# RWKV block of a four-layer trunk: four weight matrices split into two parts during the feed-forward ahead of it, and a new order for the scan's work

## The chip, the cores and the metric

One core of one Trainium2 chip runs the whole program in one launch. The metric is the device time of that launch in microseconds (us). A table below has the times of the kernel before.

## What is computed

The reference is a trunk of four layers on 256 context tokens and 256 latent tokens of width 1024. Layer 0 and layer 3 mix tokens with a gated linear recurrence (HGRN2), layer 1 with RWKV-7, layer 2 with latent attention, and each layer ends in a convolutional feed-forward part. The change touches the feed-forward of layer 0 and the RWKV mixer of layer 1:

```python
def conv_ffn(h, w_in, w_conv, b_conv, w_out):
    a, v = jnp.split(h @ w_in, 2, axis=-1)
    a = lax.conv_general_dilated(a, w_conv[:, None, :], ...) + b_conv
    return (jax.nn.silu(a) * v) @ w_out

def rwkv7_scan(r, w, k, v, kk, a, s0):
    def step(S, inp):
        rt, wt, kt, vt, kkt, at = inp
        sa = jnp.einsum('bhvk,bhk->bhv', S, -kkt)
        S = S * wt[:, :, None, :] + sa[..., None] * (kkt * at)[:, :, None, :] + vt[..., None] * kt[:, :, None, :]
        return S, jnp.einsum('bhvk,bhk->bhv', S, rt)
    ...

def project(h):                      # inside rwkv7_mixer
    ...
    r = heads(x_r @ w_rkv[0])
    k = heads(x_k @ w_rkv[1])
    v = heads(x_v @ w_rkv[2])
    g = jax.nn.sigmoid(x_g @ g1) @ g2
    ...
# readout: ((normalised y + bonus) * g) @ w_o, for both directions of the scan
```

Beside each layer the modulation of a later layer is computed: `silu(c) @ w_mod[layer] + b_mod[layer]`, a product with a matrix of 1024 x 6144.

## The kernel before

Activations lie transposed in SBUF, width on the 128 partitions and the 512 tokens along the free axis (tiles `xT`). Products in fp32 are made from three products of rounded parts: every weight and activation is split into a high part (`hi`, type fp32r) and the rest (`lo`), and `mm3` (L430) adds `hi*hi`, `hi*lo` and `lo*hi`. For weights that is done on the fly by `weights` (L414): SP loads 512 KB into `wraw` (four buffers), ACT casts it to `whi` (L426), DVE subtracts to `wlo` (L427), three buffers each.

**Feed-forward** (`ffn`, L2082): two rounds over column blocks, in each some steps over `w_in` (two blocks of columns for the gate, two for the value, 96 products of 128x512) and four over `w_out`. While it runs, `mod` loads 256 KB tiles of the next layer's `w_mod` on the SP queue (L391), eight to a step, in the first twelve steps.

**RWKV projections** (`rw_project`, L869): a norm, the six mixed inputs (`mix`), low-rank products, and two full products by `dense4`: first the keys, then the receptance. Each loads its matrix in eight chunks through `weights`, 24 products of 128x512 to a chunk. Results go to DRAM (`rwk`, `rwr`).

**RWKV scan** (`rw_scan`, L1037): the values' product (`values`, L1814) in 16 units of 12 products, whose weights come by `load` (L1821, tile `vr`), `high` (ACT, L1825) and `low` (DVE, L1829); then eight pairs of 128-column blocks, four for the context tokens and four for the latent ones. Of each pair, both directions are scanned in chunks of 64 tokens: `scaled` makes decays and keys, `products` (L1311) the chunk matrices `G`, which go through DRAM (`dg`, `inv`, `zd`) for a triangular inversion on DVE (L1404), `merge` completes the inverse on PE, `chain` runs the four dependent chunks (L1535 `r`, L1573 `v`, L1585 `k`, L1597 new state), and `readout` norms, gates and multiplies by the output matrix: SP loads `ow` (L1721), ACT makes `owh` (L1725), GpSimd (POOL) `owl` (L1729), PE the product. Between all that `modulation` (L1865) makes the modulation of two later layers in 96 units: SP loads 512 KB into `mraw`, which has one buffer (L1871), and PE makes four products of it (L1878, tile `md`).

**What sets the order.** In the feed-forward and the projections the framework orders each engine's instructions. In the scan the order is fixed by a planner in the kernel: every piece of work is a job on one engine, with a cost and a lag from `RW_COST`, delays between engines from `RW_LAT`, and a due place from the table `RW_AT`; `Jobs.schedule` (L143) simulates the engines and emits the jobs in the order of their planned starts. Each engine, and the SP and POOL queues of DMAs, then runs its own list strictly in that order. Rings (`jobs.rings`) give the number of buffers of each kind of tile. For the load of `mraw` the table has a cost of 1.46 and a lag of 1.2.

Of the kernel before, what the change touches and what calls it, by code (L numbers as in the profile page):

```python
# [51 lines left out]
RW_OW = 2  # L52
RW_M = 40
RW_LAT = {("PE", "PE"): 0, ("PE", "DVE"): 0.2, ("PE", "Act"): 0.2, ("PE", "Pool"): 0.2, ("PE", "SP"): 1.3,
          ("DVE", "PE"): 0.2, ("DVE", "DVE"): 0.127, ("DVE", "Act"): 0.13, ("DVE", "Pool"): 0.1, ("DVE", "SP"): 1.3,
          ("Act", "PE"): 0.26, ("Act", "DVE"): 0.2, ("Act", "Act"): 0.143, ("Act", "Pool"): 0.2, ("Act", "SP"): 1.3,
          ("Pool", "PE"): 0.26, ("Pool", "DVE"): 0.2, ("Pool", "Act"): 0.2, ("Pool", "Pool"): 0, ("Pool", "SP"): 1.3,
          ("SP", "PE"): 0, ("SP", "DVE"): 0, ("SP", "Act"): 0, ("SP", "Pool"): 0, ("SP", "SP"): 0}
RW_COST = {"end": 0.01, "vload": (0.73, 1.2), "vhigh": 0.52, "vlow": 0.6, "vmm": (2.62, 0.0, 6144), "vkeep": 0.48, "vout": (0.73, 1.2),
           "load": (3.6, 1.2), "norms": (0.23, 0.0, 512), "key": 0.79, "gate": (0.46, 0.0, 768), "tanh": 0.72, "affine": 0.34, "decays": 0.6,  # L60
           "exp": 0.52, "exp2": 0.62, "mul": 1.23, "ka": 0.6, "bmul": 0.6, "loadw": (0.82, 1.2), "high": 0.52, "low": 1.23,
           "heads": (0.46, 0.0, 1024), "product": (0.87, 0.0, 1024), "mask": 0.6, "out": (0.73, 1.2), "ktok": (0.43, 0.0, 512), "tok": 0.72,
           "gather": (2.3, 1.0), "ones": 0.04, "iout": (5.3, 1.5), "pair": (1.07, 0.0, 256), "keepw": 0.4, "corner": 0.63, "bturn": 0.34,
           "mfirst": (0.64, 0.0, 140), "g0": 1.04, "half": 0.53, "copy": 0.49, "turn": (0.56, 0.0, 512), "vtok": 0.8, "r": (0.29, 0.0, 512),
           "R": 0.16, "v": (0.29, 0.0, 256), "Sv": 0.32, "k": (0.29, 0.0, 512), "new": 0.78, "yg": (0.29, 0.0, 512), "sc": 0.72,
           "yx": (0.29, 0.0, 256), "yhigh": 0.52, "ylow": 0.6, "sums": (0.46, 0.0, 1024), "rs2": (3.6, -1.28), "rs3": 1.92,
           "g2": (0.92, 0.0, 1984), "wload": (0.73, 1.2), "whigh": 0.52, "wlow": 1.23, "oproj": (1.36, 0.0, 3072), "oadd": 0.6, "aout": (1.0, 1.5),
           "fin": 1.09, "xload": (0.73, 1.2), "yload": (0.73, 1.2), "res": 0.79, "mload": (1.46, 1.2), "mod": (0.49, 0.0, 1024), "mkeep": 0.48,
           "mtr": (0.43, 0.0, 512), "madd": 0.5}
RW_MAN = ("PE", "DVE", "Activation", "Pool", "SP")  # L70
RW_AT = {
# [50 lines left out]
class Jobs:  # L122
# [8 lines left out]
    def add(self, engine, name, fn, deps=(), takes=(), uses=(), tag=None, cost=None):  # L131
# [8 lines left out]
        self.list.append(x)  # L140
        return x

    def schedule(self, places, stage, lat, ordered, eps=0.05):  # L143


        free, live, ready, order = {}, {r: [] for r in self.rings}, [], []
# [2077 lines left out]
```

## Time and profile before

| | us |
|---|---|
| three runs: median (lowest to highest) | 3205.2 (3204.08 to 3209.22) |
| the profiled execution, device time | 3206.3 |
| its span, first to last instruction | 3204.4 |
| busy in the span: PE / DVE / ACT / POOL | 2886.2 / 1780.7 / 1396.0 / 496.9 |
| DMA queue of SP: data and share of the 16 engines | 377.29 MB, 38.4% |

The profile is of one execution. PE is the engine of matrix products, PEld its loading of weights, DVE, ACT and POOL the vector, scalar and GpSimd engines, SPq the DMA queue of SP. PEclk is the clock that was granted to PE, as a share of 2.4 GHz; its other level is 1.2 GHz. In lists of waits, "A <- B" says that A sat idle until B was done. In lists of groups, the idle time before a group and what ended it stand behind the bar. POOL issues no DMA in this kernel.

### The profile page before, as it was taken

Reading aid. Unit: us, or ns where it says so; the run is one execution under the profiler, and the core shown is the slowest. Engines: PE = TensorE matmul, PEld = TensorE weight load, DVE = VectorE, ACT = ScalarE, POOL = GpSimd, SP = SyncE. Lnnn points to the kernel's source line nnn. Section 1 sums busy time; section 2 is a strip of 40 time slices with the busy share of each in tenths; the row PEclk is TensorE's granted clock in tenths of the full one; section 3 lists DMA queues with packets and bytes.
Section 4 is the critical chain, followed back from the end, with each engine's and each line's share of the span. In section 5 each row is a group of like instructions: output and inputs, shape, how many; then the busy total and the mean of one; then the engine's idle time right before and its main releaser. Section 6 shows DMA issues by size and latency. Waiting matters only on the chain. (4 is left out here: it accounts for less than half of the span.)

```text
span 3204.4 us, 52055 instructions
## 1 busy us (share of the span) xinstructions
PE 2886.2 (90%) x20861; PEld 2307.1 (72%) x20861; DVE 1780.7 (56%) x3081; ACT 1396.0 (44%) x2642; POOL 496.9 (16%) x567
## 2 busy tenths in 40 slices
PE   7999999999679777878768999899989999999898
PEld 4588877778557556666547888776678887888898
DVE  4277764334674547666636434466554344488765
ACT  3266543223443345555444323245433233477544
POOL 1023200000332325344420000000000000023000
PEclk9999999999789867877878999999989999999999
DMA  7522145553264644554542333210123322322454
GB/s 277 194 68 66 51 147 171 192 158 104 81 194 133 184 126 131 154 148 139 155 140 82 96 99 96 83 48 27 40 80 99 99 92 86 93 81 81 149 184 132
DMA packets 438466, 381.33 MB, mean 119 GB/s; under 512 B 94396, under 2 KB 395346, under 8 KB 438098
## 3 DMA queue, kind: packets, MB, share of 16 engines
q1 hardware_dynamic: 436848, 377.29, 38.4%
q8 instruction: 164, 2.69, 0.4%
q10 hardware_dynamic: 1378, 0.73, 0.1%
q14 instruction: 76, 0.62, 0.1%
HBM read 354.89 MB, written 22.54 MB: 118 GB/s over the span
## 5 line engine op out<-in xcount | busy, mean ns | idle before, releaser
L427 DVE TENSOR_TENSOR wlo<-wraw,whi 128x1024 fp32r<-128x1024 f32 (+1 forms) x408 | 486.3, 1194 | 546.5 <-ACT whi L426 534.9
L433 PE MATMUL mm<-hl,whi 128*128 128x512 f32 (+1 forms) x2024 | 744.5, 368 | 10.2 <-DVE hl L528 10.2
L432 PE MATMUL mm<-hh,whi 128*128 128x512 f32 (+1 forms) x2024 | 744.1, 372 | 10.3 <-ACT hh L527 6.9
L434 PE MATMUL mm<-hh,wlo 128*128 128x512 f32 (+1 forms) x2024 | 741.0, 367 | 0.0
L426 ACT CAST whi<-wraw 128x1024 fp32r<-128x1024 f32 (+1 forms) x408 | 412.2, 1013 | 753.0 <-PE mm L433 668.0
L432 PEld LDWEIGHTS mm<-hh,whi 128*128 128x128 f32 x2024 | 385.4, 191 | 91.0 <-issue 10.0
L433 PEld LDWEIGHTS mm<-hl,whi 128*128 128x128 f32 x2024 | 385.4, 190 | 78.2 <-DVE hl L528 13.6
L434 PEld LDWEIGHTS mm<-hh,wlo 128*128 128x128 f32 x2024 | 385.1, 190 | 65.9 <-issue 6.1
L432 PE MATMUL mm<-uh,whi 128*128 128x512 f32 (+1 forms) x704 | 255.2, 363 | 0.0
L433 PE MATMUL mm<-ul,whi 128*128 128x512 f32 (+1 forms) x704 | 255.1, 363 | 0.0
L434 PE MATMUL mm<-uh,wlo 128*128 128x512 f32 (+1 forms) x704 | 254.2, 363 | 0.0
L488 POOL TENSOR_TENSOR t<-t,t 128x512 f32<-128x512 f32 (+1 forms) x27 | 35.0, 1298 | 902.8 <-ACT t L484 887.0
L1878 PE MATMUL md<-mraw,sc 128*32 128x256 f32 x768 | 74.4, 465 | 86.1 <-DMA mraw<-in_w_mod_dram 85.7
L432 PEld LDWEIGHTS mm<-uh,whi 128*128 128x128 f32 x704 | 132.7, 189 | 23.9 <-issue 2.5
L433 PEld LDWEIGHTS mm<-ul,whi 128*128 128x128 f32 x704 | 132.9, 189 | 20.4
L434 PEld LDWEIGHTS mm<-uh,wlo 128*128 128x128 f32 x704 | 132.5, 189 | 20.7
L2111 DVE SCALAR_TENSOR_TENSOR t<-mm,prm,t 128x510 f32<-128x510 f32 (+1 forms) x88 | 60.0, 682 | 139.5 <-ACT t L2109 139.5
L2109 ACT ACTIVATE t<-mm,prm 128x512 f32<-128x512 f32 (+1 forms) x88 | 63.2, 718 | 147.0 <-PE mm L434 147.0
L542 DVE SCALAR_TENSOR_TENSOR xT<-mm,mod,xT 128x256 f32<-128x256 f32 x176 | 74.6, 478 | 92.1 <-PE mm L434 92.1
L701 POOL TENSOR_TENSOR t<-t 128x512 f32<-128x512 f32 x32 | 46.4, 1449 | 361.0 <-DVE t L691 317.7
L2118 DVE TENSOR_TENSOR t<-t,mm 128x512 f32<-128x512 f32 (+1 forms) x88 | 54.4, 620 | 84.5 <-PE mm L434 84.3
L1878 PEld LDWEIGHTS md<-mraw,sc 128*32 128x32 f32 x768 | 16.5, 118 | 105.8 <-DMA mraw<-in_w_mod_dram 95.8
(418 smaller groups left out, 5167.5 us busy)
## 6 DMA issues: line engine op xcount, KB each, us to landing
wraw<-in_ffn_w_in_dram SPq DMA_DIRECT2D x176, 512.0 KB
mraw<-in_w_mod_dram SPq DMA_DIRECT2D x192, 256.0 KB
mraw<-in_w_mod_dram SPq DMA_DIRECT2D x96, 512.0 KB
wraw<-in_hg_w_in_dram SPq DMA_DIRECT2D x80, 512.0 KB
wraw<-in_ffn_w_out_dram SPq DMA_DIRECT2D x80, 512.0 KB
wraw<-in_rw_w_rkv_dram SPq DMA_DIRECT2D x16, 512.0 KB
w<-wg SPq DMA_DIRECT2D x8, 1024.0 KB
ow<-in_rw_w_o_dram SPq DMA_DIRECT2D x32, 256.0 KB
```

What stands on the lines that cost most here:

```text
L426: nc.scalar.copy(h, r)
L427: nc.vector.tensor_tensor(out=w, in0=r, in1=h.bitcast(F32), op=ALU.subtract)
L432: nc.tensor.matmul(ps, lhsT=wh, rhs=xh, start=start, stop=False)
L433: nc.tensor.matmul(ps, lhsT=wh, rhs=xl, start=False, stop=False)
L434: nc.tensor.matmul(ps, lhsT=wl, rhs=xh, start=False, stop=stop)
L488: (nc.gpsimd if k < 4 else nc.vector).tensor_tensor(out=acc[:, lo:hi], in0=acc[:, lo:hi], in1=sq[:, lo:hi], op=ALU.add)
L542: nc.vector.scalar_tensor_tensor(out=self.xT[n][:, sl], in0=ps[:, sl], scalar=m[:, which * 8 + n, s:s + 1], in1=self.xT[n][:, sl], op0=ALU ...
L701: nc.gpsimd.tensor_tensor(out=c3(de), in0=b3[:, :, end:end + 1].to_broadcast([P, 8, 64]), in1=b3, op=ALU.subtract)
L1878: nc.tensor.matmul(g["ps"][32 * c:32 * c + 32, halves[f]], lhsT=self.sc[:, k, :], rhs=g["raw", u][:, c], start=k == 0 and f == 0, stop=k = ...
L2109: nc.scalar.activation(c[:, sl], pa[b][:, sl], AF.Identity, bias=self.prm[:, cb + j + b:cb + j + b + 1], scale=w[1])
L2111: nc.vector.scalar_tensor_tensor(out=c3[:, :, 1:], in0=p3[:, :, :255], scalar=w[0], in1=c3[:, :, 1:], op0=ALU.mult, op1=ALU.add)
L2118: nc.vector.tensor_tensor(out=ss[b][:, sl], in0=ss[b][:, sl], in1=pv[b][:, sl], op=ALU.mult)
```

## The change

1. `presplit`, new: during the feed-forward of layer 0, 64 steps split the matrices of keys, receptance, values and output ahead of their use. A step loads 128x512 (256 KB) on the POOL queue into `praw`, ACT casts it to `phi`, DVE subtracts to `plo`, and two DMAs on the POOL queue store both to DRAM (`prek`, `prer`, `prev`, `preo`). `praw` and `plo` have one buffer, `phi` two.
2. `dense4`, `values` and the readout load both parts from there, with two DMAs where there was one, and no longer cast or subtract.
3. The planner gets new costs, lags and delays, a rule that keeps some DVE jobs from a start while POOL is busy (`RW_LOCK`), another threshold in its model of PE's clock, and a new table `RW_AT`; `mraw` gets a second buffer; the jobs `vhigh`, `vlow`, `whigh`, `wlow` are gone.

```diff
-RW_LAT = {("PE", "PE"): 0, ("PE", "DVE"): 0.2, ("PE", "Act"): 0.2, ("PE", "Pool"): 0.2, ("PE", "SP"): 1.3,
+RW_LAT = {("PE", "PE"): 0, ("PE", "DVE"): 0.05, ("PE", "Act"): 0.08, ("PE", "Pool"): 0.08, ("PE", "SP"): 0.05,
...
+RW_LOCK = ("affine", "bmul", "inv", "ka.0", "ka.1", "key.1", "key.2", "mask.11", "res", "rs3")
...
-                speed = 1.0 if k > 0 and busy.get(k - 1, 0.0) >= 3060 else 0.5
+                speed = 1.0 if k > 0 and busy.get(k - 1, 0.0) >= 2750 else 0.5
...
+            if x.engine == "DVE" and (x.name in locks or x.kind in locks):
+                t = max(t, port[0])
...
+    def presplit(self, st):
+
+        nc, a = self.nc, self.a
+        pool = st.enter_context(self.tc.tile_pool(name="pre", bufs=2, reuse_waits="tile"))
+        self.pre = {}
+        for n, w in (("k", a["rw_w_rkv"][0, 1]), ("r", a["rw_w_rkv"][0, 0]), ("v", a["rw_w_rkv"][0, 2]), ("o", a["rw_w_o"][0])):
+            self.pre[n] = self.dr.tile([P, 2, KT, D], F32, tag=f"pre{n}", name=f"pre{n}", bufs=1)
+            for k in range(KT):
+                for c in (slice(0, NT), slice(NT, D)):
+                    raw = pool.tile([P, NT], F32, tag="praw", name="praw", bufs=1)
+                    hi = pool.tile([P, NT], F32R, tag="phi", name="phi")
+                    lo = pool.tile([P, NT], F32R, tag="plo", name="plo", bufs=1)
+                    nc.gpsimd.dma_start(out=raw, in_=w[k * P:(k + 1) * P, c])
+                    nc.scalar.copy(hi, raw)
+                    nc.vector.tensor_tensor(out=lo, in0=raw, in1=hi.bitcast(F32), op=ALU.subtract)
+                    nc.gpsimd.dma_start(out=self.pre[n][:, 0, k, c], in_=hi.bitcast(F32))
+                    nc.gpsimd.dma_start(out=self.pre[n][:, 1, k, c], in_=lo.bitcast(F32))
+                    yield
...
+        def two(n, k0, n0):
+
+            _, hi, lo = (t.rearrange("p (a b) -> p a b", b=NT) if t is not None else t for t in self.wtiles(False))
+            for i, t in enumerate((hi, lo)):
+                nc.sync.dma_start(out=t.bitcast(F32), in_=self.pre[n][:, i, k0:k0 + 2, n0:n0 + NT])
+            return hi, lo
...
-                    wh, wl = self.weights(w[:, k0:k0 + 2, n0:n0 + NT], 2, NT)
+                    wh, wl = two(name, k0, n0)
...
-                w = g["w", u] = lp().tile([P, 2, 256], F32, tag="ow", name="ow", bufs=2)
-                nc.sync.dma_start(out=w, in_=a["rw_w_o"][0].rearrange("(k p) n -> p k n", p=P)[:, p0:p0 + 2, 256 * u:256 * u + 256])
+                w = g["w", u] = lp().tile([P, 2, 2, 256], F32R, tag="ow", name="ow", bufs=RW_OW)
+                for i in range(2):
+                    nc.sync.dma_start(out=w[:, i].bitcast(F32), in_=self.pre["o"][:, i, p0:p0 + 2, 256 * u:256 * u + 256])
...
-                x_ = V["wh"] = job("Act", "whigh", lambda u=u: whigh(u), [x_] + ([V["wh"]] if "wh" in V else []), [wh], [w])
-                x_ = job("Pool", "wlow", lambda u=u: wlow(u), [x_], [], [w, wh])
...
+                g["w", x] = vp.tile([P, 2, 4, P], F32R, tag="vw", name="vw", bufs=RW_VW)
+                for i in range(2):
+                    nc.sync.dma_start(out=g["w", x][:, i].bitcast(F32), in_=self.pre["v"][:, i, 4 * (x % 2):4 * (x % 2) + 4, x // 2 * P:x // 2 * P + P])
...
-                a_ = job("Act", "vhigh", lambda x=x: high(x), [a_], [h], [r])
-                a_ = job("DVE", "vlow", lambda x=x: low(x), [a_], [], [r, h])
...
-                t = g["raw", u] = sp.tile([P, 4, 256], F32, tag="mraw", name="mraw", bufs=1)
+                t = g["raw", u] = sp.tile([P, 4, 256], F32, tag="mraw", name="mraw", bufs=2)
...
-    def ffn(self, l, segs, mod=None):
+    def ffn(self, l, segs, mod=None, pre=False):
...
+            spl = self.presplit(st) if pre else iter(())
...
                 for j in range(j0, j1, 2):
                     next(nxt, None)
+                    steps(4)
...
                 for nb in range(0, KT, 2):
                     next(nxt, None)
+                    steps(3)
```

In the new table the load of `mraw` has a cost of 0.4 and a lag of 5.5. The call of `ffn` sets `pre` for layer 0 alone.

**Vector engine, feed-forward of layer 0** (a step over `w_in`; `plo`, `praw`, `phi` are the new split's tiles, `ul` and `uh` the activations' parts). Before:

```order
L2118 TENSOR_TENSOR t_4149<-t_4149,mm 128x512
L2118 TENSOR_TENSOR t_4155<-t_4155,mm 128x512
L427 TENSOR_TENSOR wlo<-wraw,whi 128x1024
```

Now:

```order
L2135 TENSOR_TENSOR t_4185<-t_4185,mm 128x512
L2135 TENSOR_TENSOR t_4191<-t_4191,mm 128x512
L432 TENSOR_TENSOR wlo<-wraw,whi 128x1024
L2139 TENSOR_TENSOR ul<-t_4185,uh 128x512
L2139 TENSOR_TENSOR ul<-t_4191,uh 128x512
L449 TENSOR_TENSOR plo<-praw,phi 128x512
L432 TENSOR_TENSOR wlo<-wraw,whi 128x1024
L449 TENSOR_TENSOR plo<-praw,phi 128x512
```

One new subtraction stands between nearly every two subtractions of feed-forward weights, in the same strict list; five of the 64 stand behind the feed-forward's last one, two of them among the mixed inputs of the projections.

**Tensor engine, end of the values' product** (`w<-xh,vl` and `w<-xh,vw` are its last product; `ax<-X,kb` the chunk matrices, `xg` the decay gates, `md` a modulation unit of four products, `x,G` and `xT,w` the merge of the inverse, `ident,vt` the turning of the values). Before:

```order
L434 MATMUL w<-xh,vl 128x512
L1332 MATMUL ax<-ident,kb_8122 128x128 x4
L1878 MATMUL md<-mraw,sc 32x256 x8
L1311 MATMUL ax<-X,kb_8123 128x128 x8
L1311 MATMUL ax<-X,kb_8122 128x128 x8
L1173 MATMUL ax<-xg_6742,w_8124 128x256
```

Now:

```order
L458 MATMUL w<-xh,vw 128x512
L1899 MATMUL ax<-ident,modev 128x128 x4
L1472 MATMUL ax<-x_9064,G 32x32 x32
L1889 MATMUL md<-mraw,sc 32x256 x4
L1203 MATMUL ax<-xg_7262,w_8612 128x256
L1204 MATMUL ax<-xg_7262,w_8612 128x256
```

The first pair's chunk matrices, 32 products of 128x128, now stand inside the values' product, and with them the inversion that hangs on them: what follows the values is the merge of that inverse. Before, only 16 of them stood there, and 48 (of two pairs) between the values and the chain's first `r`. Modulation units inside the values' product go from 9 to 15, those between it and the first `r` from 7 to 4.

**SP queue, one pair of the scan** (`inv<-dg` brings a pair's matrices to the inversion, `zd<-inv` takes them back; `ow` are the readout's weights). Before:

```order
L1327 DMA inv<-dg 32x16x16 x4
L1871 DMA mraw<-in_w_mod_dram 128x4x256
L1148 DMA xT_85<-rwk 128x2x256
L1149 DMA w_8124<-wg 128x8x256
L1150 DMA xT_87<-rwr 128x2x256
L1871 DMA mraw<-in_w_mod_dram 128x4x256 x2
L1637 DMA g_12350<-wo 128x3x256
```

Now:

```order
L1357 DMA inv<-dg 32x16x16 x4
L1882 DMA mraw<-in_w_mod_dram 128x4x256
L1752 DMA ow<-preo 128x2x256 x2
L1178 DMA xT_85<-rwk 128x2x256
L1179 DMA w_8612<-wg 128x8x256
L1180 DMA xT_87<-rwr 128x2x256
```

Loads of `ow`, two for each, now stand between the inversion's DMAs, where before a later place in the pair held one for each.

## Rows read from the trace of the kernel before

**Rows 1.** The page's first part: busy time, share of the span, instructions

```profile
PE 2886.2 (90%) x20861; PEld 2307.1 (72%) x20861; DVE 1780.7 (56%) x3081; ACT 1396.0 (44%) x2642; POOL 496.9 (16%) x567
```

**Rows 2.** Windows by stage: start:end, length, busy time (instructions) by engine, clock, DMA share, GB/s

```profile
486.00:820.00 334.00, 334.00 (x1550) 261.78 (x1543) 131.53 (x172) 97.06 (x123) 4.39 (x4) 1.00 0.47 151
820.00:904.00 84.00, 46.12 (x182) 37.12 (x181) 69.37 (x83) 38.53 (x62) 33.35 (x27) 0.71 0.33 92
904.00:960.00 56.00, 40.39 (x187) 33.12 (x187) 41.83 (x46) 27.31 (x39) 23.44 (x19) 0.80 0.71 233
960.00:1013.00 53.00, 53.00 (x233) 42.80 (x232) 20.00 (x19) 19.36 (x28) 5.67 (x5) 0.99 0.20 71
1013.00:1090.00 77.00, 64.26 (x339) 46.00 (x338) 31.31 (x36) 24.73 (x52) 21.09 (x36) 0.91 0.65 201
1090.00:1148.00 58.00, 33.14 (x541) 24.76 (x543) 42.55 (x88) 25.52 (x63) 20.37 (x15) 0.60 0.60 155
1148.00:1665.00 517.00, 403.12 (x6890) 308.90 (x6888) 307.65 (x680) 270.57 (x683) 205.69 (x243) 0.79 0.50 143
```

**Rows 3.** Waits of PE, 1148 to 1665: total us, times, longest

```profile
PE md L1878 <- DMA mraw<-in_w_mod_dram: 60.0, 39, 5.1
```

**Rows 4.** Waits of PE, 1090 to 1148

```profile
PE md L1878 <- DMA mraw<-in_w_mod_dram: 16.1, 3, 7.5
```

**Rows 5.** Waits of the SP queue, 1148 to 1665

```profile
SPq L1721 <- POOL owl L1729: 78.8, 21, 17.8
SPq L1871 <- PE md L1878: 76.0, 44, 10.0
```

**Rows 6.** Timeline of the SP queue in the scan: start, us, what

```profile
1305.35 0.57 SPq L1149 DMA_DIRECT2D w<-wg  x1
...
1308.89 0.37 SPq L1871 DMA_DIRECT2D mraw<-in_w_mod_dram  x1
...
1318.73 0.37 SPq L1871 DMA_DIRECT2D mraw<-in_w_mod_dram  x1
```

**Rows 7.** Timeline of PE over the same stretch, with the wait in brackets

```profile
1317.59 1.08 PE L1878 MATMUL md<-mraw,sc 128*32 128x256 f32 x8 [4.95 <-DMA mraw<-in_w_mod_dram]
1322.56 0.85 PE L1878 MATMUL md<-mraw,sc 128*32 128x256 f32 x8 [0.28 <-DMA mraw<-in_w_mod_dram]
```

**Rows 8.** Groups of instructions, 1085 to 1665: count, busy us, mean ns, idle before

```profile
L1311 PE MATMUL ax<-X,kb 64*128 64x128 f32 x480 | 51.9, 357 | 15.9 <-POOL kb L1118 8.2 <-DVE G L1315 4.1 <-DVE ro L1678 1.9
...
L1729 POOL TENSOR_TENSOR owl<-ow,owh 128x512 fp32r<-128x512 f32 x30 | 38.5, 1282 | 50.3 <-ACT owh L1725 48.2 <-PE ax L1470 2.0
...
L1725 ACT CAST owh<-ow 128x512 fp32r<-128x512 f32 x30 | 18.5, 617 | 26.2 <-PE ax L433 19.8 <-DMA ow<-in_rw_w_o_dram 2.4 <-PE ax L434 2.0
```

**Rows 9.** Groups of DVE and of ACT, feed-forward of layer 0, 486 to 820

```profile
L427 DVE TENSOR_TENSOR wlo<-wraw,whi 128x1024 fp32r<-128x1024 f32 x54 | 66.0, 1223 | 112.4 <-ACT whi L426 112.4
...
L2122 DVE TENSOR_TENSOR ul<-t,uh 128x512 fp32r<-128x512 f32 x20 | 12.9, 685 | 0.0
...
L2121 ACT CAST uh<-t 128x512 fp32r<-128x512 f32 x20 | 11.3, 614 | 0.0
```

**Rows 10.** Timeline of PE in the feed-forward: two products in a row

```profile
818.03 0.39 PE L434 MATMUL mm<-uh,wlo 128*128 128x512 f32 x1
818.26 0.39 PE L432 MATMUL mm<-uh,whi 128*128 128x512 f32 x1
```

**Rows 11.** Timeline of the SP queue: the values' first load

```profile
1013.56 0.40 SPq L1821 DMA_DIRECT2D vr<-in_rw_w_rkv_dram  x1
```

**Rows 12.** Timeline of ACT: the cast that waited for it

```profile
1016.79 0.62 ACT L1825 CAST vh<-vr 128x512 fp32r<-128x512 f32 x1 [2.98 <-DMA vr<-in_rw_w_rkv_dram]
```

**Rows 13.** Groups of DVE at the start of the projections, 836 to 904

```profile
L427 DVE TENSOR_TENSOR wlo<-wraw,whi 128x1024 fp32r<-128x1024 f32 x7 | 10.4, 1492 | 0.2 <-ACT whi L426 0.2
```

**Rows 14.** Windows of 20 us inside the scan, columns as in rows 2

```profile
1260.00:1280.00 20.00, 14.44 (x335) 12.64 (x335) 12.70 (x20) 12.08 (x25) 10.45 (x8) 0.57 0.17 53
1280.00:1300.00 20.00, 19.80 (x364) 15.51 (x363) 14.10 (x29) 14.53 (x40) 4.25 (x6) 1.00 0.60 174
```

More of the change, by code (lines that the diff above doesn't have):

```diff
@@ L52 @@
 RW_OW = 2
+RW_VW = 3
 RW_M = 40
-RW_LAT = {("PE", "PE"): 0, ("PE", "DVE"): 0.2, ("PE", "Act"): 0.2, ("PE", "Pool"): 0.2, ("PE", "SP"): 1.3,
[L55 to L69, printed above, removed]
@@ new lines @@
+RW_COST = {"end": 0.01, "vload": (0.8, 5.5), "vmm": (2.75, 0.25, 6144), "vkeep": 0.62, "vout": (0.37, 2.5), "load": (1.9, 5.5), "norms":
+    (0.43, 0.2, 256), "key": 0.9, "gate": (0.65, 0.2, 1024), "tanh": 0.87, "affine": 0.45, "decays": 1.25, "exp": 0.66, "exp2": 0.75, "mul":
+    1.3, "ka": 0.72, "bmul": 0.71, "loadw": (0.45, 5.5), "high": 0.65, "low": 1.3, "heads": (0.6, 0.25, 1024), "product": (1.09, 0.2, 2048),
+    "mask": 0.72, "out": (0.6, 2.1), "ktok": (0.46, 0.2, 512), "tok": 0.87, "gather": (2.9, 2.1), "ones": 0.07, "iout": (5, 2.5), "pair":
+    (0.64, 0.16, 256), "keepw": 0.5, "corner": 1.12, "bturn": 0.47, "mfirst": (0.61, 0.16, 140), "g0": 1.28, "half": 0.76, "copy": 0.62,
+    "turn": (0.46, 0.2, 512), "vtok": 0.77, "r": (0.29, 0.18, 512), "R": 0.3, "v": (0.29, 0.18, 256), "Sv": 0.58, "k": (0.29, 0.18, 512),
+    "new": 1.21, "yg": (0.29, 0.18, 512), "sc": 0.9, "yx": (0.29, 0.18, 256), "yhigh": 0.62, "ylow": 0.72, "sums": (0.56, 0.3, 1024), "rs2":
+    2.6, "rs3": 2.17, "g2": (1.03, 0.2, 1984), "wload": (0.8, 5.5), "oproj": (1.45, 0.2, 3072), "oadd": 0.72, "aout": (0.5, 4), "fin": 0.65,
+    "xload": (0.45, 3), "yload": (0.45, 3.5), "res": 0.92, "mload": (0.4, 5.5), "mod": (0.57, 0.3, 1024), "mkeep": 0.62, "mtr": (0.55, 0.2,
+    512), "madd": 0.5}
@@ L141, in add, with schedule @@
         return x
-    def schedule(self, places, stage, lat, ordered, eps=0.05):
-        free, live, ready, order = {}, {r: [] for r in self.rings}, [], []
+    def schedule(self, places, stage, lat, ordered, locks=(), eps=0.05):
+        free, live, ready, order, port = {}, {r: [] for r in self.rings}, [], [], [0.0]
         todo = {}
@@ L186, in start @@
                         return None
-                    t = max(t, ends[m - 1] + 0.2)
+                    t = max(t, ends[m - 1] + 0.1)
             return t
@@ L207, in schedule @@
             free[x.engine] = end
+            if x.engine == "Pool":
+                port[0] = max(port[0], end)
             ready.remove(x)
@@ L901, in mix, with dense4 @@
             return xs
-        def dense4(wap, xs, done, nxt):
-            w = wap.rearrange("(k p) n -> p k n", p=P)
+        def two(n, k0, n0):
[3 more added lines that the diff above has]
+            return hi, lo
+        def dense4(name, xs, done, nxt):
             for n0 in range(0, D, NT):
@@ L1847, in values @@
                 jobs.pair = x / 16
-                r, h = tile_of("vr"), tile_of("vh")
-                a_ = V["load"] = job("SP", "vload", lambda x=x: load(x), [V["load"]] if x else [], [r])
-                a_ = job("Act", "vhigh", lambda x=x: high(x), [a_], [h], [r])
-                a_ = job("DVE", "vlow", lambda x=x: low(x), [a_], [], [r, h])
+                h = tile_of("vw")
+                a_ = V["load"] = job("SP", "vload", lambda x=x: load(x), [V["load"]] if x else [], [h])
                 if x % 2 == 0:
@@ L2099, in ffn, with steps @@
             h = self.norm_mod(l, 1, segs, ap2(ap, 16), "h")
+            def steps(n):
+                for _ in range(n):
+                    next(spl, None)
             for j0, j1 in ((0, 12), (12, 22)):
@@ L2193, in trunk @@
                 t.mla(l, segs)
-            t.ffn(l, segs, l + 1 if l + 1 < DEPTH and l + 1 not in t.mods else None)
+            t.ffn(l, segs, l + 1 if l + 1 < DEPTH and l + 1 not in t.mods else None, (l + 1) % 3 == 1 and l + 1 < DEPTH)
         with ExitStack() as st:
```

41 lines of the change are left out of this document (15 added, 26 removed), and 73 rows, old and new, of the table RW_AT.

## The prediction

> **What bounds the kernel now.** I read the page's totals first, then busy time by stage, then the waits of the fullest engine, then single loads. Over the span PE is busy for 90% [rows 1], so a stage that the change fills with work for other engines costs nothing while PE stays full, and a stage where PE stands idle is where time can be won. The stages [rows 2] say where that is. In the feed-forward of layer 0 PE is busy for all 334 us at full clock (1.00, its 2.4 GHz level), with DVE and ACT under half full: nothing can be won there, only lost. In the projections PE has 46.1 of 84 us at first, where DVE is nearly full (69.4), then 40.4 of 56, and from 960 all of it. In the scan, 1013 to 1665, no engine is full: the values' product takes 77 us, the way to the first chain step 58 us with PE at 33.1 and a clock of 0.60, and the rest 517 us with PE at 403.1 and 0.79.
>
> So the scan is the target, and PE's waits there name one cause above all. Of the 113.9 us in which PE idles in those 517, 60.0 are 39 waits for `mraw`, the modulation's load [rows 3]; on the way to the first step another 16.1 [rows 4]. PE's list is strict, so whatever stands behind such a unit waits too. The two timelines show why. A load issued at 1308.89, 3.5 us behind 1 MB of the next pair's weights (`w<-wg`), lets PE go on at 1317.59, 8.7 us later; the next, issued at 1318.73, at 1322.56, 3.8 us later [rows 6, 7]. There is one buffer, so each load is issued only when the last unit is done (76.0 us of the queue's own waits are for that [rows 5]). The old planner put a unit 1.2 us of lag behind its load; the real gap is 3.8 us or more, and the new table has 5.5 with two buffers. The SP queue is held up further, 78.8 us, by `ow` waiting for POOL's subtraction [rows 5], a job that disappears.
>
> **The change, term by term.** The sum is made against the profiled execution (3206.3 us; the median of the three runs is 1.1 lower).
>
> *Feed-forward of layer 0: +3.* Added are 64 casts of 614 ns on ACT (39 us) and 64 subtractions of 685 ns on DVE (44 us) [rows 9]. DVE goes from 131.5 to about 175 of 334, ACT from 97.1 to 136 [rows 2]: both hidden behind PE. What could show is the queue order: a subtraction that waits for its load or for `plo`'s store holds the feed-forward's own `wlo` behind it. No DMA on POOL's queue is in this trace. The nearest row is a load of the same 256 KB on the SP queue, 3.23 us from issue to the cast that waited for it [rows 11, 12]; with cast and subtraction a step is a chain of 4.5 us. The far end is a load caught behind others, 8.7 us [rows 6, 7], and a chain of 10.0. I take the near one, since POOL's queue carries nothing but this chain, one step at a time. PE offers 334 / 64 = 5.2 us per step. Traffic: 64 x 3 x 262 KB = 50.3 MB; at 151 GB/s for a share of 0.47 [rows 2] that is 157 us more on top of 157, in 334. That nearly fills the DMA engines, so I book 3 us for late weights, with 0 and 20 as the range's ends. If PE's cover went, the whole 83 us of ACT and DVE work would compete with 24 products per chunk of 0.23 us each [rows 10], 5.4 us.
>
> *Projections: -4.* Sixteen casts and subtractions go. Seven of the subtractions stand where DVE is full, 10.4 us [rows 13]; the others lie beside a full PE or other waits and give nothing. Against that, the last two split steps spill into this stretch: two subtractions (1.4 us) and up to two waits for a load of 3.2, ACT's list standing still meanwhile, and POOL's mixed-input work standing behind the DMAs. The receptance's first chunks also bring twice the bytes into the stage whose DMA share is already 0.71 [rows 2]. Ends -10 and +10.
>
> *Values' product and the way to the first step: -25.* Today 77 + 58 = 135 us [rows 2]. DMA work in the 77 is 50 us (0.65); new are 4.2 MB of low parts and six more modulation units of 0.52 MB, 7.3 MB, at 201 GB/s / 0.65 = 309 GB/s 24 us: 74. PE has 64.3 there and gets 16 chunk-matrix products of 357 ns [rows 8], 5.7 us, and the units. Both stay under 77 but close, so I take 85. Behind it, 48 chunk-matrix products (17 us at that row's mean) leave the 58 us, the first pair's round trip through DRAM and its inversion run during the values, and 12 of the 16.1 us of `mraw` waits should go: I take 25. The sum is 110. Ends: 95 (the DMA bound plus 20) and 135 (values at 100, DMA full; 35 behind).
>
> *Rest of the scan: -55.* Removed: POOL's 30 subtractions of 1.28 us and ACT's 30 casts of 0.62 [rows 8], on engines with 205.7 and 270.6 of 517 [rows 2]; as neither is full, I book nothing for them. Moved in: 32 chunk-matrix products, 11 us, and some decay gates, 3 us. Of the 60.0 us of waits for `mraw` I expect two thirds to go, 20 staying where a load still queues behind a pair's inputs; the other 53.9 us of idle time stay. PE's 403.1 us were run at 0.79. Where PE was kept full the clock was 1.00, where it had gaps 0.57 [rows 14]; with fewer gaps I take 0.85: 403.1 x 0.79 / 0.85 = 375. Then 375 + 14 + 54 + 20 = 463 against 517, -54, rounded to -55. Ends: 0, and -95 (clock 0.95).
>
> The added SP traffic here, 32 more `ow` DMAs of 0.37 us issue time each, is 12 us on a queue that loses 78.8 us of waits. Whatever is late next is the chain itself, `r` to new state, with its hand-offs between PE, ACT and DVE.
>
> Sum: 3 - 4 - 25 - 55 = -81, from 3206.3 to 3125, or **3124** against the median.
>
> **Rivals.**
> (a) *The waits change their name.* The chain's dependencies, not `mraw`, set the pace, and PE's freed time fills with waits for ACT and DVE. For it: of the 517 us 54 are already such waits. Against: no single one of them is near 60. The rest of the scan then stays at 517: 3206 + 3 - 4 - 25 = 3180.
> (b) *The clock follows.* PE's gaps close so far that 0.95 is granted: 335 + 14 + 54 + 20 = 423, -94 in place of -55, hence 3085. For it: the full windows at 1.00 [rows 14]. Against: chains of small products always leave gaps.
> (c) *No effect.* Loads stay late in the new places, since the strict SP queue holds them behind DMAs that wait for DVE, and the values' stage reaches its far end of 135: 3204.
> (d) *Slower: the split becomes the feed-forward's bound.* One step after another hangs on the single `praw` and `plo`, in a list that DVE shares with the weights PE needs. From a step of 5.2 us on, the feed-forward grows; from (334 + 84) / 64 = 6.5 us on, it eats the whole gain of 84 behind it. If each of a step's three DMAs had to wait for one of DVE's 1.22 us subtractions [rows 9] before it could go out, a step would take 4.5 + 3.7 = 8.2 us, the stage 525 us, +191: 3206 - 84 + 191 = 3313. For it: the DMA engines nearly full, no row of a POOL DMA. Against: the near row gives 4.5.
> The Trainium skill speaks for (d): its page "SBUF — State Buffer", section "SBUF: two separate sides", says that GpSimd itself writes the descriptors of a DMA on its queue, and cannot while DVE runs an instruction in a mode that takes the port the two share. No run here shows whether these subtractions do; their 1.22 us for 1024 columns is about a column per ns, no sign of a faster mode.
>
> **How the numbers follow.** Forecast 0.60, (a) 0.15, (b) 0.12, (c) 0.05, (d) 0.08. The range goes from 3060 (the forecast's ends for the scan together with (b)) to 3190 (past (a)); it leaves out (c), (d) and a part of the tails. Under 0.2% (6 us) is taken as no change, about what three runs of this kernel spread over (5 us). Faster is forecast, (a) and (b), less 0.03 for a mishap in the projections: 0.84; same 0.06, most of (c); slower 0.10.
>
> **What would show it.** Right: PE busy for all of the feed-forward of layer 0 and still about 334 us; the first `r` about 25 us nearer to the first value product; PE's waits for `mraw` under 25 us in the scan; its clock there above 0.79; no wait for `owl` on SP. Wrong: PE waiting for `wlo` in the feed-forward with `plo` ahead of it (then (d)); a total of waits in the scan that is unchanged under other names (then (a)); DMA share near 1 in the values' stage with PE idle (then (c)).

## The result and the profile after

The changed kernel takes 3156.4 us in the median of four runs (3150.8 to 3167.1), the kernel before 3205.6 beside it: a ratio of 0.9849 with an interval of 0.9821 to 0.9877, 49 us less. Forecast were 3124 us, 81 less, in a range from 3060 to 3190: the time lies inside it, with six tenths of the gain that was forecast. In the profiled executions the span went from 3204.4 to 3152.4 us, and the 52 us can be laid out between events that both traces have (starts of instructions; v is a product of the values, r the chain's first step, the norm that of layer 2):

| | before | after | difference |
|---|---|---|---|
| to the last product of the feed-forward of layer 0 | 824.8 | 832.8 | +8.0 |
| from there to the first v | 192.7 | 192.7 | 0 |
| from the first v to the first r | 131.4 | 114.8 | -16.6 |
| from the first r to the norm | 537.7 | 492.9 | -44.8 |
| from there to the end of the span | 1517.8 | 1519.2 | +1.4 |

The windows of the changed kernel by stage, columns as in [rows 2]: the feed-forward, the values' product, the way to the first step, the scan up to where PE thins out.

```profile
489.00:833.00 344.00, 343.21 (x1592) 267.95 (x1591) 163.01 (x219) 122.52 (x169) 78.64 (x146) 1.00 0.79 260
...
1025.00:1124.00 99.00, 75.39 (x413) 49.99 (x410) 24.79 (x53) 12.31 (x26) 15.45 (x11) 0.88 0.82 233
1124.00:1140.30 16.30, 12.84 (x324) 8.47 (x322) 5.48 (x11) 14.34 (x37) 3.60 (x3) 0.90 0.64 201
1140.30:1615.00 474.70, 389.90 (x7014) 299.41 (x7010) 322.51 (x727) 268.41 (x686) 181.95 (x225) 0.85 0.60 171
```

PE is still full in the feed-forward, now at a DMA share of 0.79 (0.47 before). Its first 62 us, from the norm's first product on, ran at a lower clock than before; first the kernel before, then the changed one:

```profile
427.20:489.00 61.80, 56.83 (x263) 42.75 (x262) 39.03 (x67) 27.59 (x44) 0.00 (x0) 0.94 0.44 141
```

```profile
430.60:492.40 61.80, 56.65 (x244) 43.95 (x248) 39.74 (x69) 28.92 (x47) 11.71 (x22) 0.86 0.68 225
```

The way to the first step shrank from 58 us to 16.3, the values' product grew from 77 to 99. In the scan PE's busy time fell, with its clock at 0.85 instead of 0.79, and its idle time fell from 113.9 us to 84.8. PE's longest waits there, 1140 to 1615, answer to [rows 3]:

```profile
PE ax L1680 <- DVE ro L1675: 12.1, 5, 3.8
PE md L1889 <- DMA mraw<-in_w_mod_dram: 11.9, 8, 2.6
PE ax L1484 <- issue: 8.2, 5, 2.4
PE ax L1472 <- DVE x L1465: 7.4, 3, 3.9
PE ax L1472 <- DVE G L1345: 6.3, 2, 3.6
```

The waits for `mraw` fell from 60.0 us to 11.9; the others rose from 53.9 to 72.9. The SP queue's waits in the same stretch answer to [rows 5]: no wait for `owl`, others as long in its place.

```profile
SPq L1349 <- DVE G L1345: 61.0, 11, 11.2
SPq L1882 <- PE md L1889: 53.8, 20, 7.0
```

The steps of the new split, first its subtractions, from the timeline by tile (count, durations in ns, first and last start):

```profile
L449 DVE TENSOR_TENSOR plo<-praw,phi x64: 679/693/1761, 402.0 to 873.6; 128x512 fp32r<-128x512 f32 x64
```

Then one step on the timelines of GpSimd and ACT (start, us, what, the wait in brackets):

```profile
601.75 0.54 POOL L447 DMA_DIRECT2D praw<-in_rw_w_rkv_dram  x1
...
606.71 0.62 ACT L448 CAST phi<-praw 128x512 fp32r<-128x512 f32 x1 [4.61 <-issue]
...
607.62 0.54 POOL L450 DMA_DIRECT2D prer<-phi  x1 [5.33 <-ACT phi L448]
608.35 0.54 POOL L451 DMA_DIRECT2D prer<-plo  x1 [0.18 <-issue]
608.88 0.54 POOL L447 DMA_DIRECT2D praw<-in_rw_w_rkv_dram  x1
```

The cast started at 606.71, 5.0 us after the load's issue; over the 64 steps this takes 3.3 to 15.6 us, 5.1 in the mean. The 64 subtractions start within 472 us, one every 7.5 us in the mean: they begin 29 us ahead of the first product of the feed-forward's norm and end 41 us behind the feed-forward's last.

### The profile page after: what moved, and what is told of

It reads as the page before. It is cut to its first block, busy times and chain, and to the rows that moved or that the text cites. A ratio compares the mean times of both kernels' runs of the same rounds, so it can differ in the third digit from the quotient of the medians.

```text
span 3152.4 us, 52606 instructions
## 1 busy us (share of the span) xinstructions
PE 2875.8 (91%) x20861; PEld 2292.2 (73%) x20861; DVE 1767.0 (56%) x3113; ACT 1391.1 (44%) x2642; POOL 552.2 (18%) x727
## 5 line engine op out<-in xcount | busy, mean ns | idle before, releaser
L432 DVE TENSOR_TENSOR wlo<-wraw,whi 128x1024 fp32r<-128x1024 f32 (+1 forms) x392 | 464.7, 1188 | 428.9 <-ACT whi L431 415.6
L431 ACT CAST whi<-wraw 128x1024 fp32r<-128x1024 f32 (+1 forms) x392 | 395.9, 1013 | 554.0 <-PE mm L457 489.6
L457 PEld LDWEIGHTS mm<-hl,whi 128*128 128x128 f32 x2024 | 386.0, 191 | 79.2 <-DVE hl L552 14.4
L449 DVE TENSOR_TENSOR plo<-praw,phi 128x512 fp32r<-128x512 f32 x64 | 45.3, 709 | 171.4 <-ACT phi L448 171.3
L448 ACT CAST phi<-praw 128x512 fp32r<-128x512 f32 x64 | 39.8, 622 | 216.3 <-DMA praw<-in_rw_w_rkv_dram 119.7
```

The costliest lines, as they stand in the source:

```text
L431: nc.scalar.copy(h, r)
L432: nc.vector.tensor_tensor(out=w, in0=r, in1=h.bitcast(F32), op=ALU.subtract)
L448: nc.scalar.copy(hi, raw)
L449: nc.vector.tensor_tensor(out=lo, in0=raw, in1=hi.bitcast(F32), op=ALU.subtract)
L457: nc.tensor.matmul(ps, lhsT=wh, rhs=xl, start=False, stop=False)
```

## The experiments

Three parts of the change act on the scan: the split ahead, the second buffer of `mraw`, and the planner's new numbers (lags, costs, places, locks). The first six kernels part them.

**The split alone.** Weights split ahead, but all the planner's tables, its clock threshold and its locks (none) as before, and one buffer, in the tile and in the planner's rings:

```diff
-          ("SP", "PE"): 0.05, ("SP", "DVE"): 0.05, ("SP", "Act"): 0.05, ("SP", "Pool"): 0.05, ("SP", "SP"): 0}
+          ("SP", "PE"): 0, ("SP", "DVE"): 0, ("SP", "Act"): 0, ("SP", "Pool"): 0, ("SP", "SP"): 0}
...
-                t = g["raw", u] = sp.tile([P, 4, 256], F32, tag="mraw", name="mraw", bufs=2)
+                t = g["raw", u] = sp.tile([P, 4, 256], F32, tag="mraw", name="mraw", bufs=1)
```

> Weights split ahead as in the change, but the planner keeps its old lags, costs and places, and the modulation's weights keep one buffer. Buffer theory (the scan gained because a second modulation buffer took PE's waits for that load away, 60.0 us before, 11.9 after): the waits for the load stay at 50 to 65 us in the scan, the scan gains less than 15 us, the head of the feed-forward part and the values' stage cost what they cost in the change, 3190 to 3220 us. Split theory (the gain comes from the 64 casts and subtractions that left ScalarE, VectorE and GpSimd, and from SP no longer waiting for them, 78.8 us): most of the gain is there already, 3150 to 3170 us. Numbers theory (the gain comes from the new lags, costs and places): 3195 to 3215 us.

Measured: 3236.0 us, ratio 1.0084 (1.0057 to 1.0111), slower than before. PE's and the SP queue's waits from the first r to the norm (559.4 us, 21.7 longer than before):

```profile
PE md L1890 <- DMA mraw<-in_w_mod_dram: 65.4, 47, 4.1
```

```profile
SPq L1883 <- PE md L1890: 62.5, 43, 8.5
SPq L1753 <- PE ax L459: 59.7, 21, 19.5
```

The time lies above the ranges of all three theories. The split theory falls most plainly, and of the buffer theory the waits held: for `mraw` they are those of before, over the same two events (1148.9 to 1686.6 there):

```profile
PE md L1878 <- DMA mraw<-in_w_mod_dram: 67.8, 41, 5.1
```

SP's wait for `owl` only changed its name: `ow` must now be kept until the product is done, so its load waits for PE. Why this scan is longer than that of before, and not just as long, stays open.

**Old numbers, two buffers.**

The kernel above with the second buffer, in the tile and in the rings:

```diff
-                t = g["raw", u] = sp.tile([P, 4, 256], F32, tag="mraw", name="mraw", bufs=1)
+                t = g["raw", u] = sp.tile([P, 4, 256], F32, tag="mraw", name="mraw", bufs=2)
```

> As the kernel with the weights split ahead and the old numbers, but with the second buffer for the modulation's weights, in the tile and in the planner. Buffer theory: PE's waits for that load in the scan fall below 20 us and the time to 3155 to 3175 us, near the changed kernel. Numbers theory: the waits fall, but others come in their place, 3185 to 3210 us. Split theory: no different from the kernel with one buffer, within 5 us.

Measured: 3191.3 us, ratio 0.9957 (0.9942 to 0.9971). The scan takes 498.3 us, and its wait for `mraw` is

```profile
PE md L1890 <- DMA mraw<-in_w_mod_dram: 19.5, 18, 3.5
```

The second buffer took 61 us off the scan of the kernel with the split alone (559.4); against the scan of the kernel before (537.7) it is 39, nearly all that the change has there (492.9). The total missed the buffer theory's 3155 to 3175 and lies in the range of the numbers theory, because the way from the first v to the first r takes 143.4 us here.

**New numbers, one buffer.**

The changed kernel with one buffer, in the tile and in the rings:

```diff
-                t = g["raw", u] = sp.tile([P, 4, 256], F32, tag="mraw", name="mraw", bufs=2)
+                t = g["raw", u] = sp.tile([P, 4, 256], F32, tag="mraw", name="mraw", bufs=1)
```

> The changed kernel with one buffer for the modulation's weights, in the tile and in the planner; the order is derived anew with the new lags (a load is taken to land 5.5 us after its issue). Buffer theory: the waits for the load come back, 40 us or more in the scan, 3190 to 3215 us. Numbers theory: the planner, which now knows how long a load takes, places other work over it, waits under 20 us, 3155 to 3170 us. Split theory: 3155 to 3175 us.

Measured: 3266.2 us, ratio 1.0186 (1.0166 to 1.0206), 110 us above the change and beyond what any theory gave. The scan takes 601.8 us; PE's and SP's waits in it:

```profile
PE md L1889 <- DMA mraw<-in_w_mod_dram: 89.0, 29, 7.1
```

```profile
SPq L1882 <- PE md L1889: 98.1, 51, 6.0
```

Without the buffer the new numbers cost 30 us (3266.2 against 3236.0); with it they give 35 (3156.4 against 3191.3). The way to the first r is 116.5 us, short as in the change: that part belongs to the numbers, the scan to the buffer.

**Half loads, two half buffers.** The kernel before, each modulation load cut in two:

```diff
-                t = g["raw", u] = sp.tile([P, 4, 256], F32, tag="mraw", name="mraw", bufs=1)
+                t = g["raw", u] = sp.tile([P, 2, 256], F32, tag="mraw", name="mraw", bufs=2)
...
-                for c in range(4):
+                for c in range(2 * h, 2 * h + 2):
```

> The kernel before, with nothing split ahead and the old numbers; each load of modulation weights is cut into two of 256 KB, which take turns in two buffers of half the size (the same memory). Buffer theory: PE's waits for these loads fall from 60.0 us to under 30 in the scan, and the time by 20 to 40 us, to 3165 to 3185 us. Split theory and numbers theory: 3195 to 3215 us, since neither the splits nor the numbers changed.

Measured: 3218.7 us, ratio 1.0041 (1.0025 to 1.0056). PE's wait for the halves in the scan (537.3 us) is

```profile
PE md L1878 <- DMA mraw<-in_w_mod_dram: 62.0, 43, 10.4
```

The buffer theory missed in this form: with two buffers of half the size, 4 KB ahead as before, 62.0 of the 67.8 us stay. What helps, as the kernels with two whole buffers show, is a whole unit more in flight.

**Room for the buffer without the split.** The tile pools of the kernel before have no room for a second `mraw` of 4 KB per partition; the change gets it from `ow`, `owh`, `owl`, which shrink from 12 KB to 8. Here it comes from single buffers for `owh` and `owl`, and nothing is split ahead:

```diff
-RW_OW = 2
+RW_OW = 1
...
-                t = g["raw", u] = sp.tile([P, 4, 256], F32, tag="mraw", name="mraw", bufs=1)
+                t = g["raw", u] = sp.tile([P, 4, 256], F32, tag="mraw", name="mraw", bufs=2)
```

> The kernel before, nothing split ahead, old numbers; the room for the second whole buffer of modulation weights (4 KB per partition) is taken from the split weights of the output, one buffer each for their high and low part instead of two; the order is derived anew. Room theory (the split ahead serves mainly by the 4 KB that it frees for the second buffer): PE's waits for the modulation's load fall to 15 to 35 us after the first step of the chain, and the time to 3160 to 3190 us, as good as the split ahead with two buffers and old numbers (3191) or better. Split theory (the casts and subtractions in the scan must go as well for the second buffer to help): 3195 to 3225 us, with waits for the output's split weights in its place.

Measured: 3191.2 us, ratio 0.9958 (0.9942 to 0.9974): the time of the kernel with the split, old numbers and two buffers, 1 us past what the room theory gave. The scan takes 498.6 us (498.3 with the split). PE's and SP's waits in it, the first below the 15 to 35 us expected:

```profile
PE md L1878 <- DMA mraw<-in_w_mod_dram: 11.1, 8, 2.2
```

```profile
SPq L1721 <- POOL owl L1729: 148.9, 22, 38.0
```

SP waits nearly twice as long for `owl` as before, and the scan is as short as without that job. So neither the casts and subtractions nor SP's wait for them held the scan, and with the old numbers the split's worth for it is the 4 KB. Whether that holds with the new numbers too is not shown.

**New places, old lags.**

The changed kernel with `RW_LAT` and `RW_COST` of the kernel before, of which a part:

```diff
-    "xload": (0.45, 3), "yload": (0.45, 3.5), "res": 0.92, "mload": (0.4, 5.5), "mod": (0.57, 0.3, 1024), "mkeep": 0.62, "mtr": (0.55, 0.2,
+            "fin": 1.09, "xload": (0.73, 1.2), "yload": (0.73, 1.2), "res": 0.79, "mload": (1.46, 1.2), "mod": (0.49, 0.0, 1024), "mkeep": 0.48,
```

> The changed kernel with the new places, two buffers and the locks of VectorE, but the planner's old lags and costs. Places theory (of the 35 us between the two kernels with two buffers the places give nearly all): 3153 to 3168 us. Lags theory (the places serve only with the lags they were found for): 3175 to 3230 us, the way from the first product of the values to the first step of the chain at 130 us or more instead of 114.8.

Measured: 3223.0 us, ratio 1.0054 (1.0036 to 1.0071). The way from the first v to the first r takes 146.4 us, the scan 522.8. PE's waits, on the way behind the values' product (1080.0 to 1175.4) and in the scan:

```profile
PE md L1890 <- DMA mraw<-in_w_mod_dram: 38.0, 12, 8.9
...
PE md L1890 <- DMA mraw<-in_w_mod_dram: 35.1, 25, 6.8
```

Lags theory, in its time and in the way to the first r: the new places do not serve without the lags and costs they were found with. Which of these it is stays open. The 1.2 us for the modulation's load do not do it alone, since the old places with the same 1.2 us and two buffers left 19.5 and 11.1 us of waits for `mraw` in the scan.

**Values' weights in rows.** For the 98.5 us of the values' product:

```diff
-                for i in range(2):
-                    nc.sync.dma_start(out=g["w", x][:, i].bitcast(F32), in_=self.pre["v"][:, i, 4 * (x % 2):4 * (x % 2) + 4, x // 2 * P:x // 2 * P + P])
+                nc.sync.dma_start(out=g["w", x].bitcast(F32), in_=self.pre["v"][:, x // 2, x % 2])
```

> The changed kernel with the split weights of the values laid out in memory as they are read: each load of 512 KB is one transfer with 4 KB in a row for every partition, where the change has two transfers in rows of 512 B. Small-rows theory (the stage from the first to the last product of the values, 98.5 us in the change and 68.7 before, is held by the 512 B rows): the stage falls to 72 to 85 us and the time by 13 to 27, to 3130 to 3145 us. Bytes theory (it is held by the bytes, the twice larger loads and the 19 modulation loads beside them): 93 to 99 us, 3148 to 3160 us. Order theory (it is held by what the planner put between the products): as the bytes theory, but PE's waits for the load, 9.3 us, go.

Measured: 3171.0 us, ratio 0.9892 (0.9875 to 0.991). The window of the stage, columns as in [rows 2]; the change has a DMA share of 0.82 and 232 GB/s between the same two events:

```profile
1033.10:1130.90 97.80, 73.44 (x409) 51.06 (x410) 24.79 (x53) 12.30 (x26) 15.45 (x11) 0.87 0.74 231
```

Small-rows theory falls: the DMA engines are less busy, the bytes per second and the stage stay the same. The Trainium skill ("DMA: Bandwidth & Descriptors", section "Specifications") puts the smallest transfer for full rate at 512 B. In the traces the stage's rate is the same with either row, which agrees, but with rows of 512 B the engines were busy longer for the same bytes (0.82 against 0.74), so that these rows reach the full rate is not shown. PE's waits for `vw`, which by the order theory go, did not go either (14.4 us). The bytes theory gave the stage that came, 93 to 99 us, though the time is 11 us above its range. That the bytes hold the stage is not shown: the DMA engines are not full in it. The kernel with the new places and old lags has a short values' product, 51.0 us at the same DMA share, but with fewer of the modulation's loads beside it and with about half the products of PE in it (210 instead of 409), so it does not part the bytes from what the planner puts between the products.

```profile
1029.00:1080.00 51.00, 48.41 (x210) 37.84 (x210) 3.12 (x5) 7.91 (x16) 3.59 (x3) 0.97 0.83 249
```

The profiled execution of the kernel with rows is 13 us longer than the change's. Ahead of the first v, which comes at 1033.1 instead of 1025.5, lie 8 of them: there the split, now with stores of the values in pieces of 512 B, ends at 884 us instead of 874, and the feed-forward at 837.1 instead of 832.8. The other 5 us are in the scan.

**Output's weights in rows too.**

```diff
-                    nc.sync.dma_start(out=w[:, i].bitcast(F32), in_=self.pre["o"][:, i, p0:p0 + 2, 256 * u:256 * u + 256])
+                nc.sync.dma_start(out=w.bitcast(F32), in_=self.pre["o"][:, p0 // 2, u])
```

> As the kernel with the values' weights laid out as they are read, and the output's weights too: one transfer in rows of 4 KB for two in rows of 1 KB. Small-rows theory: another 3 to 12 us less in the scan, 3120 to 3140 us, since the modulation's loads share the DMA engines with these. Bytes theory: within 4 us of the kernel with the values alone laid out.

Measured: 3166.1 us, ratio 0.9872 (0.985 to 0.9893). This is 4.9 us below the kernel with the values alone in rows, 1 us more than the bytes theory gave, and 26 above the small-rows range. The scan takes 492.3 us, as in the change (492.9): rows of 4 KB for 1 KB show no gain.

**Split held back until after the norm.**

```diff
+                    if n == "k" and k == 0:
+                        nc.scalar.copy(raw[:, :1], h[KT - 1][1].bitcast(F32)[:, :1])
```

`h` are the normed tiles; the split is set up behind the norm in the program, too.

> The changed kernel with the first load of the weights to split held back until the norm of the feed-forward part is done (one column copied into its buffer from the last normed tile). Collision theory (the feed-forward part and what leads to it lost 7.8 us because split steps stand in the lists of ScalarE, VectorE and GpSimd ahead of the norm): the norm's first product at 427 to 428 us instead of 430.6, the last product of the part at 826 to 829 instead of 833.0, the time 3149 to 3153 us. Traffic theory (the loss is from the transfers all through the part): 3154 to 3160 us. If the steps, which keep a pace of about 7 us, now end too late for the projections, 3160 us and more.

Measured: 3186.0 us, ratio 0.9936 (0.9913 to 0.9958): the expectation's last case, 3160 us and more. The norm's first product is at 427.6 us, as before the change, the last product of the feed-forward at 828.5 instead of 832.8. But the steps end late, and the first v comes at 1058.4, 33 us later than in the change. The split's timeline and PE's waits, 833 to 905 and 905 to 1060:

```profile
L451 DVE TENSOR_TENSOR plo<-praw,phi x64: 677/692/1775, 453.1 to 934.4; 128x512 fp32r<-128x512 f32 x64
```

```profile
PE ax L519 <- POOL t L514: 12.3, 1, 12.3
...
PE ax L1015 <- ACT kp L1013: 34.1, 2, 33.4
```

In front both theories have a part: 4 of the 8 us that the change loses up to the end of the feed-forward are the steps ahead of the norm, and steps that end late stand in the lists of GpSimd and ScalarE ahead of the projections' work. ScalarE's last five casts of the split wait 5 to 11 us each for their loads, from 900 to 934 us, with the first `kp` that PE needs behind them.

**Load one step ahead.**

```diff
-                    raw = pool.tile([P, NT], F32, tag="praw", name="praw", bufs=1)
-                    hi = pool.tile([P, NT], F32R, tag="phi", name="phi")
+            if i + 1 < len(todo):
+                raws.append(load(*todo[i + 1]))
+            hi = pool.tile([P, NT], F32R, tag="phi", name="phi", bufs=1)
```

> The changed kernel with the load of each piece to split issued one step ahead: two buffers for the raw piece, one for the high part, the same memory. In the change a step takes 7.4 us (64 steps from 402 to 874 us, the last 40 us after the feed-forward part's last product at 833) and GpSimd waits 5 to 8 us in each for the piece to land and be cast, with the norm's own work behind it. Late-steps theory (the steps that end late hold up GpSimd's part of the next norm, where PE waits 6.7 us, and are what cost 34 us where they were held back by 50): a step takes 4 to 5.5 us, the last ends before 790, the wait for GpSimd falls to 0 to 4 us, and the time to 3144 to 3152 us. Crowding theory (the faster steps press on ScalarE, VectorE and the DMA queues of the part itself): the part's last product at 836 us or later, 3156 to 3175 us.

Measured: 3174.9 us, ratio 0.9898 (0.9877 to 0.992). The steps take 5.8 us and end at 769; PE's wait for GpSimd behind the feed-forward is gone, but the feed-forward itself ends at 854.2, 21 us later than in the change. PE's longest wait in it and ScalarE's waits, 430 to 855:

```profile
PE ax L403 <- ACT modev L400: 13.1, 2, 11.1
```

```profile
ACT phi L454 <- DMA prev<-phi: 58.6, 13, 8.3
...
ACT phi L454 <- DMA prer<-phi: 55.7, 15, 6.3
ACT phi L454 <- DMA preo<-phi: 35.6, 14, 6.2
```

Crowding theory, with its place: a cast waits until the one `phi` is stored, and the modulation's copy (`modev`), for which PE waits, stands behind it in the same list. From the norm's first product to the feed-forward's last PE idles for 23.8 us (6.0 in the change). This kernel was also run with the first load held back until after the norm, both edits as above:

> Both: the load one step ahead, and the first load held back until the norm of the feed-forward part is done. Late-steps theory: with steps of 4 to 5.5 us the hold costs nothing behind, and what it gave in front stays (last product of the part at 828.5 instead of 833), first product of the values at 1014 to 1020 instead of 1025.5, 3140 to 3148 us, below both kernels. Crowding theory: 3156 to 3175 us.

Measured: 3174.0 us, ratio 0.9898 (0.9877 to 0.9919), the crowding theory's range again. The feed-forward ends at 862.9, the steps at 811. In this execution layer 0's last output product already came 5 us later than in the change (433.1 against 428.0); from there to the feed-forward's end it takes 430 us, against 425 without the hold. So the hold gave nothing.

**Half pieces, two ahead.**

The kernel with the load one step ahead, with pieces of 256 columns, three buffers for each of the three tiles, and twice as many steps at each place:

```diff
-        raws = [load(*todo[0])]
+        raws = [load(*todo[i]) for i in range(2)]
...
-            hi = pool.tile([P, NT], F32R, tag="phi", name="phi", bufs=1)
+            hi = pool.tile([P, 256], F32R, tag="phi", name="phi", bufs=3)
```

> The changed kernel with the pieces to split halved (128 steps of 256 columns) and the loads issued two steps ahead, three buffers each for raw, high and low. Blocked-list theory (with the load one step ahead the feed-forward part ended 17 us later because ScalarE's casts waited 160 us in all for the one high buffer to be stored, with the part's own casts and copies behind them): those waits go, the part ends at 826 to 836, the last step ends before 800, 3144 to 3156 us. Traffic theory (the denser transfers and the larger number of casts hold the part): it ends at 845 us or later, 3160 to 3185 us.

Measured: 3158.0 us, ratio 0.9848 (0.9825 to 0.9871). ScalarE's waits for the pieces' stores are gone, the feed-forward ends at 835.2 (the kernel with the load one step ahead had it 21 us behind the change, not 17 as the expectation says), the last subtraction starts at 816, and the first v comes at 1020.9, 4.6 us earlier than in the change: the blocked-list theory, though the steps end 16 us later than it gave and the time is 2 us above its range. The profiled execution is the fastest of five, 10 us below their median. In the median this kernel is no faster than the change, whose four runs spread over 16 us. None of these versions beats the changed kernel; the kernel before with room for the buffer and the new numbers, without a split, was not tried, so whether the change needs the split at all stays open.

The planned order of the scan is the same in seven kernels, the change and the six from the values' weights in rows on: its scans took 489.1 to 498.0 us and the ways from the first v to the first r 111.0 to 115.8. So differences of 20 us and more between the orders above are real, and the 5 us between old and new numbers in the scan with two buffers are not to be read.

## Why the prediction was right, and where it was not

- *The sum.* All four terms came out worse than booked, by 5.0, 4, 8.4 and 10.2 us, and 1.4 us were added behind the scan: -52 between the profiled executions in place of -81. No errors cancelled. The range held the time because it was wide: it ended past rival (a), which stood at 3180, and the result lies about midway between the forecast and that rival.
- *What bounds the kernel.* PE's waits for `mraw` as the scan's main loss: shown. Taking the buffer away brings them back (89.0, 65.4), giving it without anything else of the change takes them away (11.1) and shortens the scan from 537.7 us to 498.6. That the SP queue "is held up further" by `owl` was a wait that cost nothing: at 148.9 us the scan is as short.
- *Feed-forward, +3: came +8.0.* Booked were late weights; of those no sign came, PE is as full as before. Of the 8.0 us, 1.1 are there before the split's first cast. Another 2.3 are the norm's first product, which waits for GpSimd's and DVE's part of the norm with the split's steps in the same lists. From there to the last product it takes 4.6 us more: PE's busy time grew by 3.6, with a clock of 0.86 instead of 0.94 in the first 62 us (0.86 to 0.92 over all kernels with the split, 0.94 in all three without), and its idle time by 1.0. Why the clock is lower there is not shown.
- *The step, 4.5 us: came 7.5.* A mis-sized term, from a load on an otherwise idle SP queue [rows 11, 12]. In the mean it takes 5.1 us from the load's issue to the cast, with the DMA engines at 0.79, then 0.9 to the subtraction, and 1.6 from there over the second store's issue to the next load; the stores' issues the sum left out. Rival (d) went wrong in its consequence: with steps above 5.2 and even 6.5 us, the feed-forward did not grow to 64 steps, since PE waits for none of the split's tiles. The steps run on into the projections. The issue of a DMA itself took 0.54 us in the median, the longest of all 0.74. The Trainium skill ("SBUF — State Buffer", section "SBUF: two separate sides") has GpSimd unable to write a DMA's descriptors while DVE runs in a mode that takes the port they share. Whether the split's subtractions run in one no run here shows, and the issues show no sign of it, so that the page speaks for (d) is not borne out.
- *Projections, -4: came 0.* PE waits 6.7 us for GpSimd's part of the norm, where the split's last steps stand, and 5.4 for the load of a modulation unit that the new order puts ahead of the first v; that took back what the work that went had given. With the last step at 816 us the stretch takes 185.6 us, 7.1 less, and with the last at 769 us 187.4: the term is there where the steps end in time.
- *Values and the way to the first step, -25: came -16.6.* The way behind the values was taken at 25 us and is 16.3; the values were taken at 85 and take 98.5. PE's 23.5 us of idle time there are nearly all waits for `mraw` and `vw`, at a DMA share of 0.82: the estimate added up the bytes, 74 us, and left 11 for all else. That the gain belongs to the new numbers is shown with the split in place: the old numbers take 131 to 148 us with one buffer or two, and the new places with the old lags 146.4.
- *Scan, -55: came -44.8.* Busy time and clock came as booked (375 + 14 = 389 at 0.85; measured 389.9 at 0.85). The waits for `mraw` fell below the 20 us expected. The step that failed is "the other 53.9 us of idle time stay": they became 72.9. That is rival (a) in part: 19 of the 48 us that went came back, 11.5 as waits for DVE, 2.5 as waits for ACT, 4.5 as idle time with no releaser that the profile shows ("issue"); waits for GpSimd did not grow.
- The planner's numbers and the buffer were booked as one. With the split and one buffer the numbers cost 30 us (3236.0 to 3266.2), with two they give 35 (3191.3 to 3156.4). With the old numbers the buffer gives 14 us without the split and 45 with it, since the split alone costs 31; both end at 3191. All together give 49.

## What to carry to other kernels

Ask of each tile that a change removes what its room will hold: here a second buffer, for which 4 KB had to be found, gave the scan's gain, and with the old numbers the work that was moved away gave none. A planner's numbers and its buffers have to be tried together: with the new numbers and one buffer this kernel lost, with two it won, and the new places without the new lags lost again. A step put beside other work needs its whole length, issues of DMAs included, and where it overruns look for who stands behind it in the same list, not at the stage it was put in.

## What was not expected

A load of 256 KB reached its cast 5.1 us after its issue in the mean, on GpSimd's queue beside a DMA share of 0.79, against 3.23 on SP's [rows 11, 12]; how much of that is the queue and how much the traffic no run parts. Rows of 512 B moved as many bytes per second as rows of 4 KB (232 and 231 GB/s) at a DMA share of 0.82 against 0.74. And a wait of 148.9 us on the SP queue cost nothing that the scan's length shows.
